# A 4096³ matmul by Strassen-Winograd products: partial sums handed on inside PSUM by ScalarE's copies, and the fifth product put ahead of the fourth

## The chip, the cores and the metric

The kernel runs on one core of one Trainium2 chip. The metric is the device time of one execution in microseconds (us), lower is better. A core has TensorE (PE in the profile: matmuls into the eight banks of PSUM, each 128 partitions x 512 fp32), VectorE (DVE), ScalarE (ACT), GpSimd (POOL) and SyncE (SP). SP, ACT and POOL also start transfers; each starts its own in order.

## The reference

```python
def reference(a, b, alpha):          # a, b: 4096 x 4096 fp32; alpha = 0.01
    x = np.matmul(a, b)
    return np.where(x > 0, x, alpha * x)
```

A full fp32 product followed by a leaky ReLU. The kernel brings a and b in as fp16 (the cast is done by GpSimd's transfers), multiplies with fp32 accumulation, and writes fp32. It also measures row norms on the way and makes a verdict (`good`, later read as `even`) on whether its method was accurate enough; if not, a plain bf16 matmul behind `tc.If(even == 0)` is run instead. For the data here it is not.

## The kernel before, in words

The output is 16 regions of 1024 x 1024. The first is made by plain matmuls during the start. The other 15 are visited in the order (0,1) (0,2) (0,3) (1,2) (1,0) (1,3) (1,1) (2,2) (2,0) (2,3) (2,1) (3,2) (3,0) (3,1) (3,3), where the first number is the row group g and the second the column group j. Each is made by one level of Strassen-Winograd: with a's and b's parts of the region cut into 2 x 2 blocks (of 512 rows or columns, 2048 deep), seven products instead of eight, with the operands of `PRODUCTS`:

- first a11·b11 and second a12·b21; their sum is the block (0,0) of the region ("u1");
- third s2·t2, added to the first in the same banks ("u2");
- fourth s3·t3 ("v"); fifth s1·t1, sixth a22·t4 and seventh s4·b22.

The s are sums of blocks of a, made once per row group by VectorE (`sum_a`, L562). The t are sums of blocks of b made for every region by VectorE in place (`b_sum`, L592). The results are put together by VectorE's additions from the banks and left through `leaky` (L313) and a store by SP. `add_v` (L1046) adds v to u2.

A product is either plain (`product`, L819: 64 matmuls 128 x 128 by 128 x 512, in four banks `y` or `z`) or is itself made by Strassen-Winograd "in quarters" (`quarter_product`, L762: 7 x 16 matmuls of 256 columns). In quarters it needs sums of its own: T1, T2 and T4 of the b operand (`sums_of_b`, L692 to L696) with T3 made in place (`t3_of_b`, L686), and four sums of the a operand, sx1 to sx4, which are made once per row group, kept in device memory (`kept_q`) and loaded again for each region (`load_sums`, L754; `following` inside the sixth loads those of the seventh on ScalarE's queue).

Which products are in quarters:

- row group 0: none;
- the first region of a later row group, (1,2), (2,2), (3,2): sixth and seventh;
- "regular" regions (`in_fourth`), (1,0) (1,3) (2,0) (2,3) (3,0) (3,1) (3,3): fourth, sixth and seventh; in (2,3), the only one in `FIFTH`, the fifth too (`fifth_in_quarters`), with its sums of s1 kept in `kept_s31` and `kept_q["s1"]`;
- "turning" regions, (1,1) and (2,1), the last of a row group (the next row group's a is brought in): the fourth.

The order of the work is written out by hand in the loop over the regions: every engine's instructions stand in program order, and what an instruction waits for is found from the tiles that it reads and writes. `y` and `z` are banks 0 to 3 and 4 to 7, exchanged from region to region. Products 0, 2 and 4 (as `product` numbers them, from 0) accumulate in y, product 1 goes to z, is added to the copy of y by VectorE (`add(u1, z)`, L1041), and z is then used by the fourth and by the sixth.

b is fetched for the next region i+1 by GpSimd (`fetch_b`, L536) into the tile of the block that the present region has read for the last time: (0,1) after the fourth, (0,0) after the sixth's code, which for (2,0) means that its buffer is free when the fifth product has been issued.

`measure` (squares on ScalarE, L231, and sums on VectorE) is put in at certain places of certain regions: before and after product 0 by `EARLY`, others by `MEASURED`. In the last region, (3,3), `judge` is called in two halves: the first, `next(judged)`, reduces the norms (L624) and moves them between partitions by two small transfers, the second, `good = next(judged)`, makes the verdict out of them with twelve small VectorE instructions (L633 to L640). The seventh product of (3,3) is `seventh_at_the_end`: each quarter product's result goes out as early as it can (L1006, L1023 and L313 on VectorE, L1010 to L1031 on ScalarE), and `even` is read from `good` between them.

In (2,2) and (3,2) T2 of the column group has been kept in device memory and is loaded instead of made (`move_t`, L518, on ScalarE's queue).

## Time and profile before

| | us |
|---|---|
| median of 3 runs | 1534.55 |
| lowest, highest | 1533.07, 1534.74 |
| span of the profiled execution | 1531.4 |
| TensorE busy | 1521.0 (99%) |
| VectorE busy | 1171.2 (76%) |
| ScalarE busy | 428.1 (28%) |
| GpSimd busy | 258.2 (17%) |

The span runs from the first to the last instruction of the profiled execution; for that execution the profile gives no other time, so the span stands for it. The profile's clock of TensorE is full in all of its 40 slices. In its rows "L819" is a line of the kernel before, "out<-in" are the tiles written and read, "ps" is PSUM, "xN" the number of instructions, and in a timeline "[1.40 <-DMA b<-in_b_dram]" tells how long the engine stood before the row and what let it go.

The profile places the regions as follows (end of the preceding region, us): (2,0) 877, (2,3) 969 (with a wait for a load at 977), (2,1) 1060.7, (3,2) 1155.9, (3,0) 1249.4, (3,1) 1341.3, (3,3) 1433.2. A regular region takes 91.9 us.

### The profile page before, as it was taken

Reading aid. Unit: us, or ns where it says so; the run is one execution under the profiler, and the core shown is the slowest. Engines: PE = TensorE matmul, PEld = TensorE weight load, DVE = VectorE, ACT = ScalarE, POOL = GpSimd, SP = SyncE. Lnnn points to the kernel's source line nnn. Section 1 sums busy time; section 2 is a strip of 40 time slices with the busy share of each in tenths; the row PEclk is TensorE's granted clock in tenths of the full one; section 3 lists DMA queues with packets and bytes.
Section 4 is the critical chain, followed back from the end, with each engine's and each line's share of the span. In section 5 each row is a group of like instructions: output and inputs, shape, how many; then the busy total and the mean of one; then the engine's idle time right before and its main releaser. Section 6 shows DMA issues by size and latency. Waiting matters only on the chain. (4 is left out here: it accounts for less than half of the span.)

```text
span 1531.4 us, 21934 instructions
## 1 busy us (share of the span) xinstructions
PE 1521.0 (99%) x8715; PEld 851.5 (56%) x8715; DVE 1171.2 (76%) x1231; ACT 428.1 (28%) x734; POOL 258.2 (17%) x426
## 2 busy tenths in 40 slices
PE   9999999999999999999999999999999999999998
PEld 4444444444446567574544747577544475746656
DVE  4378867766897676768789599688978868687677
ACT  2201334646310213103651130313464103041210
POOL 5641110143202011022220001000331100101000
PEclk9999999999999999999999999999999999999999
DMA  9999995998979999899898939859999892948824
GB/s 248 188 216 200 239 281 168 180 193 176 251 312 257 277 237 276 243 290 246 184 310 279 302 149 231 294 154 343 217 241 297 229 347 70 295 161 189 302 97 140
DMA packets 194258, 356.50 MB, mean 233 GB/s; under 512 B 18913, under 2 KB 132833, under 8 KB 181090
## 3 DMA queue, kind: packets, MB, share of 16 engines
q0 software_dynamic: 119808, 112.22, 46.4%
q1 hardware_dynamic: 67714, 217.22, 38.0%
q10 hardware_dynamic: 6624, 25.56, 4.4%
q8 instruction: 70, 1.15, 0.3%
q14 instruction: 42, 0.34, 0.1%
HBM read 347.61 MB, written 117.44 MB: 304 GB/s over the span
## 5 line engine op out<-in xcount | busy, mean ns | idle before, releaser
L819 PE MATMUL ps<-b,a 128*128 128x512 f16 x2624 | 570.7, 379 | 1.4 <-DMA b<-in_b_dram 1.4
L819 PE MATMUL ps<-b,s 128*128 128x512 f16 x2176 | 475.2, 379 | 0.0
L819 PEld LDWEIGHTS <-a 128*128 128x128 f16 x2624 | 256.7, 98 | 309.3 <-issue 1.7
L819 PEld LDWEIGHTS <-s 128*128 128x128 f16 x2176 | 212.8, 98 | 255.2 <-issue 0.4
L592 DVE TENSOR_TENSOR b<-b 128x4096 f16<-128x4096 f16 x104 | 234.8, 2286 | 46.0 <-DMA b<-in_b_dram 34.1
L536 POOL DMA_DIRECT2D b<-in_b_dram x128 | 94.8, 745 | 879.8 <-PE ps L762 448.2
L832 ACT COPY c<-ps 128x512 f32<-128x512 f32 x164 | 85.0, 596 | 483.2 <-PE ps L819 439.2
L142 DVE STREAM_TRANSPOSE a<-a 128x512 uint32<-128x512 uint32 (+2 forms) x120 | 127.0, 1105 | 78.9 <-DMA a<-in_a_dram 78.9
L133 POOL DMA_DIRECT2D a<-in_a_dram x252 | 137.4, 553 | 245.5 <-ACT junk L611 73.6
L762 PEld LDWEIGHTS <-q 128*128 128x128 f16 x1488 | 145.6, 98 | 16.9
L313 DVE SCALAR_TENSOR_TENSOR c<-c 128x1024 f32<-128x1024 f32 (+2 forms) x123 | 141.8, 1194 | 4.1 <-ACT c L832 3.8
L611 ACT ACTIVATE junk<-a 128x512 bf16<-128x512 f16 x192 | 121.1, 631 | 83.4 <-DMA a<-in_a_dram 78.1
L1041 DVE TENSOR_TENSOR c<-ps,c 128x512 f32<-128x512 f32 x140 | 87.5, 683 | 62.8 <-PE ps L819 51.2
L231 ACT ACTIVATE sq<-b 128x2048 bf16<-128x2048 f16 x64 | 118.4, 1910 | 38.8 <-DVE sq L240 31.0
L762 PEld LDWEIGHTS <-a 128*128 128x128 f16 x1200 | 117.4, 98 | 17.4
L283 PE MATMUL ps<-b,a 128*128 128x512 f16 x512 | 112.2, 379 | 0.5 <-ACT a L380 0.2
L762 PE MATMUL ps<-b,q 128*128 128x256 f16 x816 | 95.6, 273 | 0.0
L762 PE MATMUL ps<-b,a 128*128 128x256 f16 x752 | 88.3, 273 | 0.0
L283 PEld LDWEIGHTS <-a 128*128 128x128 f16 x512 | 49.7, 98 | 60.8 <-issue 1.4
L977 ACT COPY c<-ps 128x512 f32<-128x512 f32 x9 | 5.3, 586 | 255.6 <-PE ps L762 145.8
L762 PEld LDWEIGHTS <-s 128*128 128x128 f16 x672 | 65.7, 98 | 7.6
L762 PE MATMUL ps<-q,q 128*128 128x256 f16 x544 | 64.6, 273 | 0.0
(108 smaller groups left out, 917.0 us busy)
## 6 DMA issues: line engine op xcount, KB each, us to landing
b<-in_b_dram POOLq DMA_DIRECT2D x136, 512.0 KB, 11.8
out_dram<-c SPq DMA_DIRECT2D x240, 256.0 KB, 7.0
a<-in_a_dram POOLq DMA_DIRECT2D x244, 128.0 KB, 5.7
b<-kept_half SPq DMA_DIRECT2D x28, 1024.0 KB, 11.8
b<-kept SPq DMA_DIRECT2D x20, 1024.0 KB, 8.8
q<-kept_qs ACTq DMA_DIRECT2D x40, 512.0 KB, 7.8
s<-kept_s SPq DMA_DIRECT2D x18, 1024.0 KB, 7.6
q<-kept_qa SPq DMA_DIRECT2D x28, 512.0 KB, 7.5
```

What stands on the lines that cost most here:

```text
L133: nc.gpsimd.dma_start(a16[32 * q:32 * q + 32], src.rearrange("(g i) w -> i g w", i=32))
L142: nc.vector.transpose(part.rearrange("p c m e -> p c (m e)").bitcast(U32) .rearrange("p c (g i) -> p g c i", i=32), src[:, :, i * n:(i + 1 ...
L231: nc.scalar.activation(to, self.parts[n], SQUARE)
L283: nc.tensor.matmul(ps, a_cols(at[0, h, u], c, mt, (h, u) == (0, 0)), bt[0, u, nt][:, c, :], start=first, stop=last,)
L313: nc.vector.scalar_tensor_tensor(t, t, alpha, t, op0=MULT, op1=MAX if alpha <= 1 else MIN)
L536: nc.gpsimd.dma_start(t[:, c:c + 4, :], b_rows(j, u, c, 4, nt, g > 0))
L592: nc.vector.tensor_tensor(f(to), f(x0), f(x1), op)
L611: nc.scalar.activation(junk, piece[:, q, :], SQUARE, accum_out=to[:, 4 * n + q:4 * n + q + 1])
L762: nc.tensor.matmul(to[m], xq[:, c // 2, rows, c % 2], yq[:, c, :], start=first and c == 0 and m < banks, stop=c == KC - 1, skip_group_chec ...
L819: nc.tensor.matmul(banks[mt], a_cols(t, c, mt, t is first_a), B(half, nt, k)[:, c, :], start=first and (k, c) == todo[0], stop=(k, c) == t ...
L832: nc.scalar.copy(kept[mt], banks[mt])
L1041: nc.vector.tensor_add(to, bank, to)
```

## The change

- **FIFTH is gone.** `fifth_in_quarters`, `kept_s31` and `kept_q["s1"]` are removed; every fifth product is plain.
- **Seeds.** After product 0, ScalarE copies the four banks y into z (bank to bank), product 1 is accumulated on these (`product(1, z, False)`), and u1 is read out by four ScalarE copies (`keep(z, side)`) instead of VectorE's `add(u1, z)`. In the turning regions of row groups 1 and 2 the sixth product starts in the same way on copies of u2, and is copied back. To give the copies time, the last 16 matmuls of product 0 (and of product 2 in regular regions) and the first 16 of product 1 (and of product 4) run bank by bank.
- **EARLY measures.** Only the first one ends before the copies; others begin after the copies and end after the b sums.
- **Regular regions, order.** Both units of t4, the sixth's operand (made in B(1,0)), are summed after product 1 instead of one of them after product 2; the first of the two units of t1, the fifth's operand (made in B(0,0)), is summed during product 2, followed by T3, T2 and T1 of the fourth, and then the second unit. Then comes product 4 (the fifth, plain, in y) directly after product 2, `fetch_b(i + 1, [(0, 0)])` directly after it, and only then the fourth (`fourth_by_seeds`). `fetch_b(i + 1, [(0, 1)])` stays behind the fourth.
- **Fourth and sixth by seeds.** In both, intermediate sums go from bank to bank by ScalarE's copies (`nc.scalar.copy(one, chain)`), so that VectorE adds 2 parts rather than 5 in the fourth; the quarter products and sums of the sixth stand in another order. The kept sums of a22 are loaded one after product 2, two within the fourth, one near its end.
- **judge.** `good = next(judged)` stands after the sixth instead of before the fifth; T4 for the seventh of (3,3) is made at the end of the sixth; `even` is read one quarter product later.

The loads of T2 in (2,2) and (3,2) are not edited, but stand in program order behind the four seed copies on ScalarE.

```diff
-    FIFTH = {(2, 3)}
-    kept_s31 = dram_pool.tile([P, QUARTER], DT, name="kept_s31")
...
+            if n == 0 or n == 2 and in_fourth:
+                order[-16:] = [(mt, k, c) for mt in range(MT) for k, c in todo[-4:]]
+            elif n == 1 or n == 4 and in_fourth:
+                order[:16] = [(mt, k, c) for mt in range(MT) for k, c in todo[:4]]
             if n == 0 and late_s2:
...
+        def fourth_by_seeds(banks, tq, sx, sq, late):
+
+            pairs, kept = new_c(side)
+            b = quarters_of_b(i, 0, 1)
+            x = quarters_of_a(g, "s3")
+            chain, shared, one, other = banks
             t = lambda n: b_quarter(tq[n])
...
+            quarter_product(x[0, 0], b[0, 0], into(chain), True)
+            nc.scalar.copy(one, chain)
+            quarter_product(sx[1], t(1), into(shared), True)
+            quarter_product(sx[2], t(2), into(chain))
+            nc.scalar.copy(other, chain)
+            quarter_product(x[0, 1], b[1, 0], into(one))
+            nc.scalar.copy(block(0, 0), pair(one))
+            for n in (2, 3):
+                sq[n] = new_a16()
+            load_sums("a22", sq, (2, 3))
+            quarter_product(sx[3], b[0, 1], into(chain))
+            nc.scalar.copy(one, chain)
+            nc.scalar.copy(block(1, 1), pair(chain))
+            quarter_product(sx[4], b[1, 1], into(other))
+            nc.scalar.copy(block(0, 1), pair(other))
+            sq[4] = sq["room"] = late
+            load_sums("a22", sq, (4,))
+            quarter_product(x[1, 1], t(4), into(one))
+            nc.scalar.copy(block(1, 0), pair(one))
+            return pairs, kept, [(block(r, 1), pair(shared)) for r in (1, 0)]
...
+            quarter_product(x[0, 0], b[0, 0], into(chain), True)
+            nc.scalar.copy(one, chain)
+            add(v, y)
+            quarter_product(sx(1), t(1), into(shared), True)
             following(4)
             next_t[2] = tq[1]
...
+            leave(v_pairs, 1, 1)
+            quarter_product(sx(2), t(2), into(chain))
+            nc.scalar.copy(other, chain)
             following(2)
...
             sums_of_b(y7, next_t, (2,))
...
+            quarter_product(x[0, 1], b[1, 0], into(one))
+            more(0, 0, one)
+            for r in (0, 1):
+                more(r, 1, shared)
+            next_t[4] = tq[2]
+            if not final:
+                sums_of_b(y7, next_t, (4,))
+            quarter_product(sx(3), b[0, 1], into(chain))
+            nc.scalar.copy(one, chain)
+            more(1, 1, chain)
+            following(1, sq.get("last"))
             quarter_product(sx(4), b[1, 1], into(other))
...
             more(0, 1, other)
+            following(3, sq.get("room"))
+            quarter_product(x[1, 1], t(4), into(one))
             more(1, 0, one)
...
+            sums_of_b(y7, next_t, (1, 4) if final else (1,))
             return next_t, next_s
...
             leaky(block(0, 0))
-            even = nc.values_load(good[0:1, 0:1], min_val=0, max_val=1)
             quarter_product(sx(2), t(2), ones)
...
             leaky(block(0, 1))
+            even = nc.values_load(good[0:1, 0:1], min_val=0, max_val=1)
             quarter_product(sx(3), b[0, 1], ones, by_row=True)
...
         product(0, y, True)
...
+        for m in early[:1]:
             m.end()
+        for mt in range(MT):
+            nc.scalar.copy(z[mt], y[mt])
+        for m in early[1:]:
+            m.begin()
...
-        product(1, z, True)
+        product(1, z, False)
...
-        add(u1, z)
+        u1_pairs, _ = keep(z, side)
         leave(u1_pairs, 0, 0)
...
         for k in ks:
             b_sum(B(0, 0, k), B(1, 1, k), B(0, 0, k), SUB)
+            if in_fourth and k == ks[0]:
+                tq = {n: new_a16() for n in (2, 1)}
+                y7 = quarters_of_b(i, 0, 1)
+                t3_of_b(y7)
+                sums_of_b(y7, tq, (2, 1))
...
+            sq = {1: new_a16()}
+            load_sums("a22", sq, (1,))
+            product(4, y, False)
+            fetch_b(i + 1, [(0, 0)], ks)
+            t3_of_b(y6)
+            sums_of_b(y6, t6, (2, 1))
+            t3_of_b(quarters_of_b(i, 1, 1))
+            v_pairs, v, parts = fourth_by_seeds(z, tq, {**s3_rooms(g), 4: a_quarter(sx4)}, sq, t[:, 3])
+            for to, bank in parts:
+                nc.vector.tensor_add(to, bank, to)
+            add_v()
+            tq = t6
+            sums_of_b(y6, tq, (4,))
...
-        if final and not in_fifth:
-            good = next(judged)
...
-            product(4, y, False)
+        if not in_fourth:
+            product(4, y, False)
...
+            tq, sq = sixth_in_quarters(u2_pairs, banks, v_pairs, v, y, tq, sq)
+            if final:
+                good = next(judged)
...
-            product(5, z, g > 0)
-            add(u2[::-1], z[::-1])
+            product(5, z, False)
+            if g:
+                for mt in range(MT):
+                    nc.scalar.copy(u2[mt], z[mt])
+            else:
+                add(u2[::-1], z[::-1])
```

More of the change, by code (lines that the diff above doesn't have):

```diff
@@ L846, in fourth_in_quarters @@
             nc.scalar.copy(block(0, 0), pair(one))
-            if not turning:
-                quarter_product(sx[4], b[1, 1], into(other), True)
             quarter_product(x[1, 1], t(4), into(third), True)
@@ L907, in sixth_in_quarters @@
+        def sixth_in_quarters(pairs, banks, v_pairs, v, y, tq, sq):
             b = quarters_of_b(i, 1, 0)
             x = quarters_of_a(g, "a22")
-            one, other, third, fourth = banks
+            chain, shared, one, other = banks
             t = lambda n: b_quarter(tq[n])
@@ L1104 @@
             keep_s2(g)
-        if i and regions[i - 1] in FIFTH:
-            for c in range(KC // 2):
-                nc.sync.dma_start(by_chunk(x21(g, "a22"))[:, c], by_chunk(kept_s31)[:, c])
         product(0, y, True)
@@ L1121 @@
                 move_t("t2", t, k, False, nc.scalar)
-        u1_pairs, u1 = keep(y, side)
         if middle:
@@ L1136 @@
             middle.end()
+        for m in early[1:]:
+            m.end()
         if g == 1 and j in OTHERS:
```

168 lines of the change are left out of this document (26 added, 142 removed).

## The prediction

> **What bounds the kernel now.** I read the page first, then TensorE's waits, the chain of waits that ended last, and VectorE's timeline over the last region. The page:
>
> ```profile
> span 1531.4 us, 21934 instructions
> PE 1521.0 (99%) x8715; PEld 851.5 (56%) x8715; DVE 1171.2 (76%) x1231; ACT 428.1 (28%) x734; POOL 258.2 (17%) x426
> PEclk9999999999999999999999999999999999999999
> ```
>
> TensorE works through 99% of the span at full clock. A change can only gain by fewer matmul columns or by the few microseconds in which TensorE stands; it can lose in every new wait. TensorE's waits, with total, count and longest in us:
>
> ```profile
> PE ps L819 <- DMA b<-in_b_dram: 1.4, 1, 1.4
> PE wp L106 <- DVE x L92: 1.2, 1, 1.2
> ...
> ```
>
> The second, and two more that are not shown (each smaller), belong to the start. Only the first is in the range of the change. The chain says what it is (start, length, what):
>
> ```profile
> 945.38 33.41 DMA b<-in_b_dram
> 978.79 0.04 issue
> 978.84 32.97 PE ps L819 x152
> 1011.80 48.94 PE ps L762 x448
> ...
> 1114.41 110.51 PE ps L819 x512
> ...
> 1433.23 41.44 PE ps L819 x192
> 1474.67 12.23 PE ps L762 x112
> 1486.90 13.81 PE ps L819 x64
> 1500.71 22.72 PE ps L762 x208
> ...
> 1525.77 0.42 DVE c L313
> ```
>
> After the load that lands at 978.79 (B(0,0) of region (2,3)) there is no gap on TensorE up to 1523. Here are the prices too: a plain product of 64 matmuls is 13.81 us, one in quarters (112 matmuls of half the width) 12.23 us, so one quarter product is 12.23 / 7 = 1.747 us. From 978.84 on, L762 x448 is four products in quarters in a row: the fourth to seventh of (2,3).
>
> **The change, part by part.** The sum is made against the profiled execution of 1531.4 us; the median of the runs, 1534.55, stands 3.15 us above that span, and I add the sum to the median.
>
> *The fifth of (2,3) becomes plain.* 13.81 − 12.23 = +1.58 us on TensorE, which nothing covers. With it go 4 stores and 4 loads of s1's sums, the kept part of s3, and some VectorE work that covered nothing on the path: no gain from them.
>
> *The fetch of the next B(0,0) moves up.* GpSimd's timeline:
>
> ```profile
> 944.65 1.48 POOL L536 DMA_DIRECT2D b<-in_b_dram  x2 [5.43 <-PE ps L819]
> ```
>
> The pair could issue only when the fifth product, the last reader of B(0,0), was nearly through. The fifth now stands ahead of the fourth, so the pair issues about 12.2 us earlier. Even with the same 33.4 us in flight it lands near 967, ten before the need at 977.4: −1.4 us. The (0,1) pair, which went out ahead of it, now goes after the fourth, about 12 to 14 later; it is first read by the sums for the third product, so 33 us in flight still suffice.
>
> *Seeds from product 0 to 1.* In each of 15 regions four ScalarE copies put y into z, product 1 accumulates on them, and four copies out replace four VectorE additions. The rows for these:
>
> ```profile
> L832 ACT COPY c<-ps 128x512 f32<-128x512 f32 x164 | 85.0, 596 | 483.2 <-PE ps L819 439.2
> L1041 DVE TENSOR_TENSOR c<-ps,c 128x512 f32<-128x512 f32 x140 | 87.5, 683 | 62.8 <-PE ps L819 51.2
> 876.60 18.73 PE L819 MATMUL ps<-b,a 128*128 128x512 f16 x86
> 885.07 1.91 ACT L231 ACTIVATE sq<-b 128x2048 bf16<-128x2048 f16 x1 [1.79 <-DVE sq L240]
> 888.27 7.31 ACT L231 ACTIVATE sq<-b 128x2048 bf16<-128x2048 f16 x4 [1.29 <-DVE sq L243]
> 895.49 2.03 ACT L832 COPY c<-ps 128x512 f32<-128x512 f32 x4
> ```
>
> No row shows a copy from bank to bank; its nearest is bank to SBUF, .596 each and four in 2.03, and I take that. The last 16 matmuls of product 0 and the first 16 of product 1 go bank by bank, so bank m ends 4 × .216 = .86 us after bank m−1 and is wanted .86 after its neighbour: every copy has about 3 × .86 = 2.6 us, in regions that keep the order by pairs of banks about 1.7, against .6 plus handing over. Cost 0; if a copy took 1.1 us, the second pair's two would end 1.1 and 2.2 after product 0 and be wanted at 1.73 and 2.59: still in time. The danger is ScalarE's other work: in (2,0), whose product 0 (876.60 + 13.81) ends at 890.4, the copies of y stood behind eight squares of `measure`, 5.1 us late, and as seeds they would hold TensorE for that long. But the changed kernel ends only the first measure ahead of the copies (squares to 886.98) and begins the second (888.27) behind them; the first pair of banks is complete at about 887.0. That VectorE has four additions of .683 fewer gains nothing: TensorE doesn't wait for it there.
>
> *Fourth by seeds.* The same 112 matmuls, with three bank-to-bank copies, each having one quarter product (1.747) to hide in .6. Cost 0. Its a22 quarters are loaded later: two right after the fourth's third and second operands are through, one at its end, each about 10.4 us ahead of its use. Median landing of such loads:
>
> ```profile
> q<-kept_qs ACTq DMA_DIRECT2D x40, 512.0 KB, 7.8
> q<-kept_qa SPq DMA_DIRECT2D x28, 512.0 KB, 7.5
> DMA to landing us min/median/max: 3.0/7.8/11.1
> ```
>
> So 0 at the median, up to .7 at the maximum.
>
> *Sixth by seeds.* VectorE's timeline in region (3,3) gives the spacings, here and for the tail (two additions of 512 columns in 1.29, so .60 apart; a half-size sum 1.13 apart; two leaky ReLU in 2.35):
>
> ```profile
> 1488.14 0.36 DVE L624 TENSOR_REDUCE ends<-stats 128x2 f32<-128x32 f32 x3
> ...
> 1494.34 2.35 DVE L1046 TENSOR_TENSOR c<-c 128x1024 f32<-128x1024 f32 x2
> 1496.61 0.59 DVE L633 TENSOR_REDUCE most<-line 1x2 f32<-1x256 f32 x1
> ...
> 1499.65 0.15 DVE L640 TENSOR_TENSOR good<-ok 1x1 int32<-1x1 f32 x1
> 1500.10 1.29 DVE L1041 TENSOR_TENSOR c<-ps,c 128x512 f32<-128x512 f32 x2 [0.30 <-PE ps L819]
> ...
> 1513.60 1.22 DVE L696 TENSOR_TENSOR q<-b,q 128x2048 f16<-128x2048 f16 x1
> 1514.73 2.36 DVE L313 SCALAR_TENSOR_TENSOR c<-c 128x1024 f32<-128x1024 f32 x2
> 1517.00 0.75 DVE L1006 TENSOR_TENSOR c<-ps,c 128x256 f32<-128x256 f32 x2
> ...
> 1520.02 1.29 DVE L1023 TENSOR_TENSOR c<-ps,c 128x512 f32<-128x512 f32 x2 [1.54 <-DMA out_dram<-c]
> ```
>
> In the sixth the margin is thin. Its seventh quarter product accumulates on the bank that ScalarE may overwrite only after VectorE has read it (`more(0, 0, one)`). VectorE has other work ahead of that read. Counted from the sixth's start, and with those spacings: the second half of `add_v` can begin at .83, once the fourth's last copy (.6) is out, and ends at 1.96; T4 3.1; four additions of y at .60 each 5.5; the leaky ReLU of v (2 × 1.13) 7.77; T2 8.9; the read 9.5. ScalarE's copy ends at 10.2, and TensorE arrives at 6 × 1.747 = 10.48. Margin .2 to .3, in six regions: cost 0, up to .5 each if one link is longer.
>
> *T2 loads of (2,2) and (3,2).* They stand on ScalarE's queue behind the four seeds, and so go out only after product 0:
>
> ```profile
> 1167.18 0.33 ACTq L518 DMA_DIRECT2D b<-kept_t  x1
> 1169.69 0.33 ACTq L518 DMA_DIRECT2D b<-kept_t  x1
> DMA to landing us min/median/max: 4.8/8.9/12.0
> ```
>
> Region (3,2) starts three plain products after the chain's 1114.41, at 1155.85; its product 0 ends at 1169.67 and product 2 reads them at 1183.5; leaving at about 1170.9 behind the seeds, with 12.0 in flight, they land at 1182.9. Cost 0, with little to spare at the maximum.
>
> *The turning regions' sixth product* starts on seeds from u2: four more copies within product 5's 13.81. Cost 0.
>
> *The tail.* In region (3,3) the verdict of `judge` (`good = next(judged)`) moves from before the fifth's end to behind the sixth, ahead of the leaky ReLU of u2. In the rows above, twelve small instructions from 1496.61 to 1499.80 are 3.2 us that VectorE had free. On TensorE:
>
> ```profile
> 1500.55 1.91 PE L762 MATMUL ps<-b,a 128*128 128x256 f16 x16
> ...
> 1512.78 3.66 PE L762 MATMUL ps<-b,s 128*128 128x256 f16 x32
> ```
>
> It starts the sixth at 1500.55 and the seventh 12.23 later, at 1512.78. VectorE reads y's first two banks at 1517.00 to 1517.75 (L1006); TensorE's fifth quarter product of the seventh (`onto(0, 1)`) writes these banks at 1512.78 + 4 × 1.747 = 1519.77: a margin of 2.0.
>
> After the change, counted from the sixth's start, VectorE has: `add_v`'s second half from .83 to 1.96; T4 to 3.10; L624 .28, to 3.38; four additions of y 2.4, to 5.78; leaky of v 2.27, to 8.04; T2 to 9.17; five additions from banks at .6, to 12.2; the sixth waits for the last quarter product, 12.49 to 13.09; T4 and T1 2.26, to 15.35; judge 3.22, to 18.57; leaky of u2 2.27, to 20.84; L1006 twice, to 21.6. TensorE would want the banks at 12.23 + 6.99 = 19.22, so it stands about 2.4. VectorE's rest (two more pairs, L1023, four leaky, four additions, about 7.3 with no room between) ends at 28.57, against 1526.19 − 1500.55 = 25.64 before. The end comes +2.93 us later; the last stores follow as before. Bounds: 0 if VectorE is not the bound, 3.2 if all of judge shows, plus some tenths for the later `values_load`.
>
> Sum: 1.58 − 1.4 + 2.93 = +3.1 us: 1534.55 + 3.1 = 1537.7.
>
> One rule of the skill bears on the new stall. The trace: TensorE's 1.4 us wait at 977.4 left the clock at 9 in every slice, and at the start 11 matmuls of 512 columns took 4.11 us, .37 each, where 64 in 13.81 later take .216:
>
> ```profile
> 1.19 4.11 PE L106 MATMUL wp<-w 128*128 128x512 f16 x11 [1.19 <-DVE x L92]
> ```
>
> The Trainium skill, "TensorE: Matmul & The Clock Gate", section "What's actually happening", says that the clock halves after an idle window of some 3.4 us. By it a stall of 2.4 costs itself alone, and the sum stays; one longer than 3.4 would have the rest at half speed.
>
> **The rivals.**
>
> *A, forecast:* the tail is late, the rest is hidden: 1537.7, from 1536.6 to 1538.6.
>
> *B, new waits in the regular regions besides.* For it: margins of .2 to .3 in the sixth, of .7 for the loads, in six or seven regions. Against it: VectorE is at 76%, and the waits need the slow end of their rows. At .3 to .5 in seven regions: +2.1 to +3.5, 1539.8 to 1541.2.
>
> *C, the other side: the tail is covered.* If VectorE reads y's first two banks within 6.99 us of the seventh's start, then TensorE doesn't stand and the end stays: 1.58 − 1.4 = +.2, 1534.7. It decides at 2.4 us less on VectorE between the sixth's start and that read, for instance if the additions to u2 come one quarter product earlier than I count. Against: each term is a row of this same region.
>
> *D, the clock falls in the tail.* A stall beyond 3.4 us, with the last three quarter products (5.24) at half speed: +1 +5.2, 1543.9. It needs a stall one us longer than worked out.
>
> *E, faster:* the 1.4 us are got back, more stalls that I don't see go too, and the tail is covered. TensorE's only other gaps are the start's; there is nothing to win 3 us from.
>
> **How the numbers follow.** 0.2% is 3.07 us, about what a measurement of this kernel can tell from no change: the bounds are 1531.5 and 1537.6. Chances: A .53, B .20, C .21, D .03, E .03. A lies on the upper bound, so I give it half and half, .25 same and .28 slower; B and D are slower, C is the same: faster .03, same .46, slower .51. The range goes from C, 1534.5, to B's upper end, 1541.0.
>
> **What would show it.** TensorE's busy time from 8715 to 8667 matmuls, and the wait of 1.4 for b<-in_b_dram gone; a wait of about 2.4 us of TensorE for VectorE's additions to c in the last 10 us; judge's twelve small instructions (L633 to L640) some 15 us into the sixth and the seventh; VectorE's last leaky ReLU about 3.1 later than 1525.77 + .42. Wrong would be: TensorE waits for ScalarE at product 1, or for the copies in the sixth, or for q<-kept_qa, in several regions (B); no wait in the tail (C); a granted clock under 9 in the last slice (D).

## The result, and the profile after

The changed kernel takes 1536.79 us (median of 20 runs, 1536.40 to 1538.65). The kernel before takes 1532.39 us over 20 runs made beside them (1531.29 to 1538.32), lower than each of the three runs that the prediction could see (they are among the 20). The ratio is 1.0025 with a 95% interval of 1.0018 to 1.0032, so the change makes the kernel slower by 3.8 us (2.8 to 4.9; 4.4 by the medians). Predicted were +3.1 us.

The first lines of the page after:

```profile
span 1535.9 us, 21828 instructions
PE 1523.3 (99%) x8667; PEld 846.8 (55%) x8667; DVE 1093.0 (71%) x1104; ACT 495.6 (32%) x857; POOL 258.2 (17%) x426
```

VectorE has 78 us less to do, ScalarE 67 us more, and TensorE 2.3 us more in its records (48 matmuls fewer, but wider). TensorE's waits after (total, count, longest in us):

```profile
PE ps L758 <- DVE c L977: 1.6, 1, 1.6
PE turned L373 <- DVE a_rounded L357: 1.2, 1, 1.2
...
PE ps L283 <- DVE a L142: 0.8, 1, 0.8
```

The wait of 1.4 for b<-in_b_dram is gone. One of 1.6 for VectorE is new. The other two lie in the first 100 us, in the region of the start, whose code the change leaves alone; the wait of 0.8 varies from profile to profile (0 to 1.2 in those below). The chain's end, in which no wait stands between regions any more:

```profile
1434.39 55.25 PE ps L819 x256
1489.64 22.71 PE ps L758 x208
1512.38 1.91 PE ps L758 x16
1514.31 7.16 PE ps L758 x64
1521.47 1.20 DVE c L313
```

55.25 us are now four plain products in a row (the fifth ahead of the fourth), and at 1521.47 the chain leaves TensorE for VectorE, where before it stayed on TensorE up to 1523.43. TensorE's and VectorE's timelines there:

```profile
1501.70 1.91 PE L758 MATMUL ps<-b,a 128*128 128x256 f16 x16
...
1514.31 3.65 PE L758 MATMUL ps<-b,s 128*128 128x256 f16 x32
1517.80 3.66 PE L758 MATMUL ps<-q,q 128*128 128x256 f16 x32
1523.06 3.87 PE L758 MATMUL ps<-b,q 128*128 128x256 f16 x32 [1.60 <-DVE c L977]
```

```profile
1510.99 4.03 DVE L900 TENSOR_TENSOR c<-ps,c 128x512 f32<-128x512 f32 x6
...
1517.20 0.59 DVE L633 TENSOR_REDUCE most<-line 1x2 f32<-1x256 f32 x1
...
1520.25 0.15 DVE L640 TENSOR_TENSOR good<-ok 1x1 int32<-1x1 f32 x1
1520.33 2.34 DVE L313 SCALAR_TENSOR_TENSOR c<-c 128x1024 f32<-128x1024 f32 x2
1522.60 0.73 DVE L977 TENSOR_TENSOR c<-ps,c 128x256 f32<-128x256 f32 x2
...
1529.44 0.42 DVE L313 SCALAR_TENSOR_TENSOR c<-c 128x256 f32<-128x256 f32 x1
```

From 1501.70, the sixth's start, VectorE has no pause until the end of L977. The verdict (L633 to L640) begins 15.5 us after that start, and the leaky ReLU of u2 can follow only at 1520.33; TensorE, which could have gone on at 1521.30, starts its fifth quarter product of the seventh at 1523.06.

The whole difference of the two profiled executions (1535.9 − 1531.4 = 4.5 us) can be laid out by three points of each trace: the sixth's start in (3,3), VectorE's last instruction, and the end of the span.

| | sixth's start | to VectorE's end | from there to the end | span |
|---|---|---|---|---|
| before | 1500.55 | 25.64 | 5.2 | 1531.4 |
| after | 1501.70 | 28.16 | 6.0 | 1535.9 |
| difference | +1.15 | +2.52 | +0.8 | +4.5 |

The first term lies in the start: the first matmul of L819 begins at 120.51 us before and at 121.77 after, and in the other profiles anywhere from 120.42 to 122.31. From there to the sixth's start the two take 1380.0 and 1379.9 us, so that the plain fifth and the lost wait cancel. The second term is the tail that the prediction has. The third is not in its sum (its bounds allow some tenths for the later reading of `even`). In the experiments below, profiles that keep the tail of the kernel before have 4.2 to 4.9 us there, those that keep the changed kernel's have 5.9.

A run's time is longer than its span, and not by the same amount in each kernel: by 1.9 us in the 20 runs of the changed kernel (median span 1534.9), by 2.5 to 3.0 us, as medians, in the four sets of runs of the kernel before that stand beside the experiments (median spans 1529.6 to 1530.3). In spans the change therefore costs some 5 us, in time 3.8 to 4.4. What fills the part outside the span is not in the traces.

### The profile page after: what moved, and what is told of

It is laid out like the page before. It is cut to its first block, busy times and chain, and to the rows that moved or that the text cites. A ratio compares the mean times of both kernels' runs of the same rounds, so it can differ in the third digit from the quotient of the medians.

```text
span 1535.9 us, 21828 instructions
## 1 busy us (share of the span) xinstructions
PE 1523.3 (99%) x8667; PEld 846.8 (55%) x8667; DVE 1093.0 (71%) x1104; ACT 495.6 (32%) x857; POOL 258.2 (17%) x426
## 3 DMA queue, kind: packets, MB, share of 16 engines
q8 instruction: 70, 1.15, 0.3%
## 4 chain that ended last, share of the span: by engine, by line
PE 96%; DMA 2%; DVE 1%; POOL 1%; issue 0%; ACT 0%; SPq 0%; DVEq 0%
PE ps L819 68%; PE ps L758 23%; PE ps L283 4%; DMA a<-in_a_dram 1%; DMA b<-in_b_dram 1%; POOL b L193 0%; DMA a_in<-in_a_dram 0%; POOL a L133 0%; DVE a L142 0%; DVE c L977 0%; DVE c L313 0%; PE turned L373 0%; DVE c L993 0%; DVE a L380 0%; DVE part L320 0%
## 5 line engine op out<-in xcount | busy, mean ns | idle before, releaser
L819 PE MATMUL ps<-b,a 128*128 128x512 f16 x2624 | 570.6, 379 | 0.0
L819 PE MATMUL ps<-b,s 128*128 128x512 f16 x2240 | 488.0, 379 | 0.0
L819 PEld LDWEIGHTS <-a 128*128 128x128 f16 x2624 | 256.7, 98 | 307.7
L819 PEld LDWEIGHTS <-s 128*128 128x128 f16 x2240 | 219.2, 98 | 263.8
L536 POOL DMA_DIRECT2D b<-in_b_dram x128 | 94.8, 745 | 873.3 <-PE ps L819 402.2
L832 ACT COPY c<-ps 128x512 f32<-128x512 f32 x164 | 86.0, 596 | 285.6 <-PE ps L819 273.0
L758 PEld LDWEIGHTS <-q 128*128 128x128 f16 x1424 | 139.3, 98 | 18.1 <-issue 2.0
L758 PE MATMUL ps<-b,q 128*128 128x256 f16 x784 | 92.0, 273 | 1.7 <-DVE c L977 1.6
L1080 ACT COPY ps<-ps 128x512 f32<-128x512 f32 x60 | 32.8, 572 | 163.0 <-PE ps L819 163.0
L1184 DVE TENSOR_TENSOR c<-ps,c 128x512 f32<-128x512 f32 x14 | 9.7, 691 | 105.8 <-ACT c L878 102.2
L1012 DVE TENSOR_TENSOR c<-ps,c 128x512 f32<-128x512 f32 x72 | 44.5, 679 | 45.8 <-PE ps L819 45.8
L758 PE MATMUL ps<-q,q 128*128 128x256 f16 x640 | 73.1, 273 | 0.0
```

The source lines that it names most:

```text
L536: nc.gpsimd.dma_start(t[:, c:c + 4, :], b_rows(j, u, c, 4, nt, g > 0))
L758: nc.tensor.matmul(to[m], xq[:, c // 2, rows, c % 2], yq[:, c, :], start=first and c == 0 and m < banks, stop=c == KC - 1, skip_group_chec ...
L819: nc.tensor.matmul(banks[mt], a_cols(t, c, mt, t is first_a), B(half, nt, k)[:, c, :], start=first and (k, c) == todo[0], stop=(k, c) == t ...
L832: nc.scalar.copy(kept[mt], banks[mt])
L1012: nc.vector.tensor_add(to, bank, to)
```

## The experiments

Each run's time stands beside runs of the kernel before on the same chip.

### The fifth product made plain, and nothing else

```diff
-    FIFTH = {(2, 3)}
+    FIFTH = set()
```
(on the kernel before)

> The kernel before with FIFTH empty and nothing else: the fifth of (2,3) becomes plain. My theory: 13.81 - 12.23 = +1.6 us, nothing hides it, and the wait of 1.4 us for B(0,0) stays: 1534.0 where the kernel before has 1532.4. The rival: the quarters' additions and loads cost as much somewhere as they save on TensorE: 1532.4.

Measured: 1532.88 us, ratio 0.9996 (0.9988 to 1.0005). The rival has it: the same time. TensorE's wait of 1.4 us is gone in this profile too, although here the fetch of B(0,0) stands where it stood. The rows for its four transfers in the kernel before and in this one are the last lines of two views of line L536, between 937 and 948 us:

```profile
DMA to landing us min/median/max: 16.5/25.9/33.4
```

```profile
DMA to landing us min/median/max: 6.3/9.1/12.4
```

They are issued 0.65 us apart in the two traces, and the last lands in 12.4 us instead of 33.4. What else is on its way at that time in the kernel before, on SyncE's queue:

```profile
929.15 7.04 SPq L710 DMA_DIRECT2D kept_qs<-q  x4
936.61 6.43 SPq L754 DMA_DIRECT2D q<-kept_qa  x4
```

The four stores of 512 KB are the sums of s1 that the quartered fifth of (2,3) needs. Without it they aren't made, and the loads behind them go out earlier. So in these two profiles the quartered fifth saves 1.58 us in (2,3) and costs as much at the start of the same region (1.4 us of wait, 1.56 in the spacing of TensorE's matmuls). Which of the transfers that go away or go earlier had slowed the pair, this run does not separate.

The wait is not the same in every execution. In the profile of the run with the late verdict below, whose edit does not touch it, it is 3.2 us. The shortest span of the kernel before is 1528.8 us, as short as that of the last run below, in whose profile this wait is gone, while the shortest here is 1530.4. By these spans (an estimate, since only one execution of each kernel has a trace) the fastest executions of the kernel before have no such wait and keep the 1.58 us. The times do not show it, since here they exceed the spans by 2.0 us, and by 2.8 in the runs of the kernel before beside them.

### The fetch of B(0,0) put back

```diff
             product(4, y, False)
-            fetch_b(i + 1, [(0, 0)], ks)
             t3_of_b(y6)
...
-        if not in_fourth:
-            fetch_b(i + 1, [(0, 0)], ks)
+        fetch_b(i + 1, [(0, 0)], ks)
```

> The changed kernel with the fetch of the next region's B(0,0) put back behind the sixth's code, so that it stands behind the (0,1) pair on GpSimd's queue. My theory: the wait of 1.4 us at the start of (2,3)'s product 0 comes back, or a longer one, 1.4 to 3 us: 1538.2 to 1539.8. The rival (the wait went because other loads went, not because this fetch goes out earlier): no wait, 1536.8.

Measured: 1644.85 us, ratio 1.0725. The direction is as expected, the size is not: 108 us. Of these 78.0 are waits of TensorE for b, and TensorE is busy for 30.6 us longer (1553.9 instead of 1523.3), at a mean granted clock of 0.972 instead of 0.999. The changed kernel's GpSimd in (2,0), then TensorE's wait in this run and the landing of the pairs issued between 970 and 978 us:

```profile
926.67 1.48 POOL L536 DMA_DIRECT2D b<-in_b_dram  x2 [71.32 <-DVE b L684]
933.58 1.48 POOL L536 DMA_DIRECT2D b<-in_b_dram  x2 [5.43 <-PE ps L819]
942.56 2.98 POOL L536 DMA_DIRECT2D b<-in_b_dram  x4 [7.50 <-PE ps L758]
```

```profile
PE ps L819 <- DMA b<-in_b_dram: 78.0, 19, 6.4
```

```profile
DMA to landing us min/median/max: 5.3/27.4/50.0
```

With the fourth behind the fifth, the (0,1) tiles come free only near the region's end, and in program order the (0,0) transfers now stand behind them. Eight transfers go out within 6 us and the last takes 50 us to land. In the changed kernel the (0,0) pairs go out 16 and 9 us before the (0,1) pairs, and nothing waits. The new order of the products therefore depends on the new place of the fetch, even though that place was not needed to lose the old 1.4 us.

### Two tries with an early verdict

In the first, both halves of `judge` are moved ahead:

```diff
+            if final:
+                judged = judge(b_pool.tile([1, P * 6], FP32, name="line", tag="b12"))
+                next(judged)
             product(4, y, False)
...
             t3_of_b(quarters_of_b(i, 1, 1))
+            if final:
+                good = next(judged)
             v_pairs, v, parts = fourth_by_seeds(...)
...
-            if final:
-                good = next(judged)
```

> The changed kernel with both halves of judge moved ahead: the first half before the fifth product of (3,3), the verdict before the fourth's additions, where VectorE stands idle for 15.49 us. My theory (the tail: 3.2 us of judge ahead of the leaky ReLU of u2 hold VectorE, and through the banks TensorE): TensorE's wait of 1.6 us at the end goes, VectorE ends 2.5 to 3.4 us earlier, and the time is 1533.4 to 1534.3 where the changed kernel has 1536.8. The rival (the extra time comes from new waits in other regions, or from the start): the time stays within 0.5 of 1536.8.

Measured: 1536.96 us, ratio 1.0021 (1.0012 to 1.0029): as the rival has it, but for another reason. VectorE and TensorE in this run:

```profile
1500.38 0.60 DVE L633 TENSOR_REDUCE most<-line 1x2 f32<-1x256 f32 x1 [15.64 <-DMA line<-lines]
```

```profile
1504.96 3.65 PE L758 MATMUL ps<-q,q 128*128 128x256 f16 x32 [0.97 <-DVE c L1189]
...
1515.54 1.91 PE L758 MATMUL ps<-q,a 128*128 128x256 f16 x16 [1.69 <-ACT ps L925]
```

The tile `line` takes the room of a b tile that the fourth reads to its end, so its transfer waited for the fourth, and VectorE stood for 15.64 us in front of the verdict. The 3.2 us fell on the sixth instead of the seventh: TensorE waits at 1504 and 1514 and no longer at 1521. The second try gives `line` another room:

```diff
-                judged = judge(b_pool.tile([1, P * 6], FP32, name="line", tag="b12"))
+                room = x_pool.tile([P, 4, QUARTER], DT, name="q", tag="x")
+                judged = judge(room[:1, 0, :P * 12].bitcast(FP32))
```

> As the first run with an early verdict, but the small transfer of judge goes to a tile that is free when the fifth product ends (in the first run its tile was still held by the fourth product, so the verdict came at 1500.38 and held the sixth). The verdict now falls in VectorE's idle time. My theory (judge at the tail costs all of VectorE's delay): no wait of TensorE for VectorE in the last 40 us, VectorE ends 25.6 us after the sixth's start instead of 28.2, and the time is 1533.4 to 1534.5. The rival (the tail's cost is in the sixth's new order, and not in judge): TensorE doesn't wait, but the end stays within 0.7 of the changed kernel's 1536.8.

Measured: 1534.12 us, ratio 1.0008 (0.9999 to 1.0017), within the expectation of the theory and 2.7 us below the changed kernel. Two rows of VectorE:

```profile
1490.67 0.60 DVE L633 TENSOR_REDUCE most<-q 1x2 f32<-1x256 f32 x1 [6.85 <-DMA q<-lines]
...
1516.46 2.35 DVE L313 SCALAR_TENSOR_TENSOR c<-c 128x1024 f32<-128x1024 f32 x2
```

The verdict lies in idle time, TensorE doesn't wait anywhere after the start, and VectorE ends 25.75 us after the sixth's start at 1501.16, 0.1 us more than in the kernel before. The tail of the prediction is judge, and not the sixth's new order.

### The verdict made twice, and half again

```diff
+        for again in range(2):
+            good = verdict(by, again)
+        yield good
...
```

> The changed kernel with the verdict's twelve small instructions made twice, so 3.2 us more on VectorE at the same place. If judge is on the path that sets the end: TensorE's wait at the end grows from 1.6 to about 4.9 us, and the time by 3.2 to about 1540.0. If it is not on it: 1536.8. If TensorE's clock falls after a stall of this length, as the Trainium skill, TensorE: Matmul & The Clock Gate, section What's actually happening, has it for an idle window of some 3.4 us: the three quarter products after the stall (5.24 us) take up to twice as long, and the time is up to 1545.

Measured: 1542.53 us, ratio 1.0051 (1.0037 to 1.0064). The time grows by 4.0 us (by the ratios) to 5.7 (by the medians) over the changed kernel's, and not by 3.2. TensorE, and its clock in a stretch of 3.3 us behind the wait (the column after POOL's busy time):

```profile
1526.62 5.54 PE L763 MATMUL ps<-b,q 128*128 128x256 f16 x32 [4.71 <-DVE c L982]
```

```profile
1527.30:1530.60 3.30, 3.30 (x18) 2.36 (x16) 2.27 (x5) 0.00 (x0) 0.00 (x0) 0.50 0.46 169
```

32 matmuls take 5.54 us instead of 3.66, and the granted clock is 0.50: to the 3.2 us of the verdict comes a slower clock behind a stall of 4.9. VectorE ends 4.6 us later after the sixth's start than in the changed kernel, so the clock costs about 1.4. A stall between this one and the changed kernel's 1.8 is made by repeating only the verdict's three reductions:

```diff
-        for t, n, op in ((most, 0, MAX), (least, 1, MIN), (total, 2, ADD)):
-            nc.vector.tensor_reduce(t, by[:, n], axis=X, op=op)
+        for again in range(2):
+            for t, n, op in ((most, 0, MAX), (least, 1, MIN), (total, 2, ADD)):
+                nc.vector.tensor_reduce(t, by[:, n], axis=X, op=op)
```

> The changed kernel with the verdict's first three reductions made twice: 1.57 us more on VectorE at the tail, so that TensorE's stall there is about 3.3 us, between the 1.8 us after which its matmuls kept their spacing and the 4.9 us after which 31 of them took twice as long. If the stall alone counts: the time grows by 1.6, to 1538.4. If a stall shorter than the 3.4 us of the Trainium skill, TensorE: Matmul & The Clock Gate, section What's actually happening, is enough, as the wait of 2.2 us in the kernel before with the late verdict has it: some 15 to 31 matmuls at .213 instead of .109 us, and 1540 to 1542.

Measured: 1538.67 us, ratio 1.0036 (1.0022 to 1.0049).

```profile
1523.79 5.54 PE L759 MATMUL ps<-b,q 128*128 128x256 f16 x32 [3.17 <-DVE c L978]
```

The time fits the first expectation (1538.4) and the trace the second: the clock falls here too, and 32 matmuls take 5.54 us. In the profile VectorE ends 31.25 us after the sixth's start, 3.1 later than in the changed kernel, 1.6 of it for the reductions and 1.5 for the clock; but only 4.1 us follow instead of 6.0, by which time SyncE has long taken its branch (at 1525.5). (The wait of 2.2 us that the expectation names is in the run that follows.)

### The kernel before with the late verdict

```diff
-        if final and not in_fifth:
-            good = next(judged)
...
             tq, sq = sixth_in_quarters(...)
+            if final:
+                good = next(judged)
```

> The kernel before with the verdict alone moved behind the sixth. Its leaky ReLU of u2 then ends at about 1520.2 instead of 1517.0, TensorE's fifth quarter product of the seventh waits about 1.2 us for VectorE, and VectorE ends about 1.8 us later: 1534.3 where the kernel before has 1532.5 (1533.7 to 1535.6). If judge is not what delays the tail: 1532.5.

Measured: 1535.98 us, ratio 1.0028 (1.0016 to 1.0040): the direction is right, and the size is 3.7 us by the medians instead of 1.8. TensorE's waits and two rows of its timeline:

```profile
PE ps L819 <- DMA b<-in_b_dram: 3.2, 1, 3.2
PE ps L762 <- DVE good L640: 2.1, 1, 2.1
...
PE ps L762 <- DVE q L694: 0.7, 1, 0.7
```

```profile
980.76 9.40 PE L819 MATMUL ps<-b,a 128*128 128x512 f16 x35 [3.20 <-DMA b<-in_b_dram]
...
1523.10 2.48 PE L762 MATMUL ps<-q,q 128*128 128x256 f16 x16 [2.08 <-DVE good L640]
```

In the kernel before, `even` is read out of `good` between the second and the third quarter product of the seventh, and TensorE reads it too. So TensorE waits for `good` itself, ahead of the banks that I had in mind: 2.1 us. That wait was enough for the clock to fall:

```profile
1524.30:1527.50 3.20, 3.20 (x17) 2.27 (x15) 1.88 (x4) 0.65 (x2) 0.00 (x0) 0.50 0.62 221
```

That would be a reason to read `even` a step later, as the change does; no run has the changed kernel with the reading at its old place. The profile's own 1539.9 us hold a longer wait at 978 as well (3.2 us, followed by a stretch at half clock: 35 matmuls in 9.40 us, .27 each).

### When the branch is taken

With the verdict early and clear, VectorE ends as in the kernel before, but in its profile 6.4 us go by from there to the end of the span, against 5.2. SyncE's rows at line 1305 (the branch on `even`) in that run, and its last stores in it and in the kernel before:

```profile
L1305 SPq EVENT_SEMAPHORE  x8: 17/17/17, 1523.6 to 1524.1; - x8
...
L1305 SPq COMPARE_BRANCH  x1: 50/50/50, 1520.9 to 1520.9; - x1
```

```profile
1524.29 4.08 SPq L1339 DMA_DIRECT2D out_dram<-c  x4
```

```profile
1523.11 3.44 SPq L1393 DMA_DIRECT2D out_dram<-c  x4
```

From the branch at 1520.9 to SyncE's next instruction at 1523.6 pass 2.7 us. The Trainium skill, "Runtime: NRT & Kernel Launch", section "Instruction fetch mechanics", has it that a branch to a place outside the prefetched instructions waits until these are fetched; the gap fits that, though no run shows the fetch. The first store's data was ready at 1523.8, and it left at 1524.29. The test reads `even` earlier:

```diff
-            even = nc.values_load(good[0:1, 0:1], min_val=0, max_val=1)
...
+        if final:
+            even = nc.values_load(good[0:1, 0:1], min_val=0, max_val=1)
         leave(u2_pairs, 1, 0)
```

> The run with the early, clear verdict, and even is read out of good before the stores of u2 instead of between the quarter products of the seventh. In that run SyncE read good for 0.75 us behind u2's stores, branched for 2.6 us, and issued the first of the last stores 0.5 us after its data was ready; the last store left 0.7 us after VectorE's last instruction. My theory (the branch on SyncE's queue is what the changed tail still costs beside judge): the last stores go out as VectorE ends, and the time falls by 0.5 to 1.0 us from 1534.1 to about 1533.3, within 1 us of the kernel before. The rival (what is left comes from the start or from transfers): 1534.1 stays.

Measured: 1533.13 us, ratio 1.0002 (0.9993 to 1.0011), as the theory has it, 1.0 us below the run before it. The two intervals overlap, so the number alone does not settle it; the profile agrees, with 4.4 us from VectorE's end to the end of the span. In the changed kernel this path was longer still: u2's stores leave later by the whole delay of the leaky ReLU, and SyncE reads, branches and stores behind them, so that its last four stores begin at 1528.18, 1.3 us after the first one's data (the leaky ReLU of 1526.15) could have gone:

```profile
1528.18 2.46 SPq L1338 DMA_DIRECT2D out_dram<-c  x4
```

The other try on this path starts from the early, clear verdict (the "run before it" of its expectation) and cuts the last four stores in halves:

```diff
-    for to, t in last:
-        nc.sync.dma_start(to, t)
+    for n, mts in ((0, (0, 1)), (1, (0, 1)), (1, (2, 3)), (0, (2, 3))):
+        for mt in mts:
+            to, t = last[mt]
+            cols = slice(n * HALF, (n + 1) * HALF)
+            nc.sync.dma_start(to[:, cols], t[:, cols])
```

> As the run before it, with the last four stores of 256 KB made as eight of 128 KB, in the order in which their halves are finished. If the time after VectorE's last instruction (5.2 us in the kernel before, 6.0 in the changed one) depends on the size of the last store: about 1 us less, 1532.4 to 1533.5. If it is a fixed latency: the same as the run before it.

Measured: 1535.87 us, ratio 1.0022 (1.0012 to 1.0031). Neither expectation: by the medians it is 1.75 us slower than with whole stores, though the two intervals overlap. VectorE ends as early (25.75 us after the sixth's start), but 7.0 us go by behind it instead of 6.4. SyncE takes .35 us and more for each store (median .56), so that the last of the eight goes out 4.1 us after VectorE's last instruction, where the last of the four goes out after 0.7. That explains 0.6 of the 1.75 us; the rest stays open.

### The seeds of product 1 undone

```diff
-        for mt in range(MT):
-            nc.scalar.copy(z[mt], y[mt])
+        u1_pairs, u1 = keep(y, side)
...
-        product(1, z, False)
+        product(1, z, True)
...
-        u1_pairs, _ = keep(z, side)
+        add(u1, z)
```

> The changed kernel with the seeds of product 1 undone alone: y is copied out by ScalarE, product 1 starts afresh in z, and VectorE adds z to the copy (4 additions of 0.68 in each region). My theory, that handing the banks on by copies costs TensorE nothing: within 0.5 of the changed kernel's 1536.8, or up to 1 us more where VectorE's 2.4 us per region make a sum late. The rival, that the seeds hold TensorE: 1534 to 1536.

Measured: 1538.29 us, ratio 1.0035 (1.0022 to 1.0048), 1.5 us above the changed kernel (the intervals overlap) and half a microsecond beyond the range of my theory; the rival, that the seeds hold TensorE, falls. If undoing them costs something, part of it is that VectorE's 2.4 us in each region come back in front of a sum that the fifth product of (2,0) needs:

```profile
PE ps L819 <- DVE b L592: 0.4, 1, 0.4
```

That wait is .4 of the 1.5 us. From the first matmul of L819 to the sixth's start in (3,3) this profile takes .6 us longer than the changed kernel's. The rest stays open.

### The kernel before without its wait, and with the fifth in quarters

If the wait of 1.4 us came from traffic, the kernel before could keep the quarters and lose the wait:

```diff
-            fetch_b(i + 1, [(1, 0)], (1, 0) if in_quarters else ks)
+            if not s1_here:
+                fetch_b(i + 1, [(1, 0)], (1, 0) if in_quarters else ks)
         leave(u2_pairs, 1, 0)
+        if s1_here:
+            fetch_b(i + 1, [(1, 0)], (1, 0))
```

> The kernel before with one transfer moved: in (2,0) the loads of the next region's B(1,0) from kept_half (2 MB) go behind the stores of u2. The fifth of (2,3) stays in quarters. My theory (the wait of 1.4 us came from traffic: the four stores of s1's sums and these loads slow the last pair of B(0,0), 33.4 us in flight where it takes 12.4 us without the stores): the pair lands before its need, the wait goes, and the time falls by 1.5 us to about 1530.8, below both kernels. The rival (the kept stores alone decide, or the wait moves to B(1,0)): the time stays at 1532.3 or grows.

Measured: 1532.40 us, ratio 0.9995 (0.9986 to 1.0004). The last pair of B(0,0) lands in 28.3 us instead of 33.4, in time, and the wait at 978 is gone. But TensorE now waits in (2,1):

```profile
PE ps L762 <- DVE q L694: 1.8, 1, 1.8
```

VectorE makes T4 there behind transposes of the next row group's a, which wait for transfers; TensorE comes 1.4 us earlier and meets it. One more move puts the last of these transposes behind T2, T4 and T1:

```diff
-        if g:
-            bring_a(0, 0, [3])
+        if turning and g:
+            fetch_a(0, 0, 3)
...
             sums_of_b(quarters_of_b(i, 0, 1), tq, (2, 4, 1))
+            turn_a_in(0, 0, 3)
```

> The run with the later half loads, in whose profile the wait at 978 was gone but TensorE waited 1.8 us at 1104 in (2,1) for T4 of the fourth (VectorE, L694), plus one more move: in the turning regions (1,1) and (2,1) the last transposes of the next row group's a (L142, 2.1 us) go behind T2, T4 and T1 of the fourth. If the gain at 978 was lost at 1104 alone: T4 is ready 2.1 us earlier, no wait is left, and the time is 1530.8, below both kernels. If it is lost again further on (the later squares on ScalarE, or the next pieces of a): 1532.4 stays.

Measured: 1532.90 us, ratio 1.0002 (0.9993 to 1.0012). In its profile no wait of TensorE is left outside the first 100 us, and the span is 1530.3, the shortest of all. The median does not follow. Whether other executions of it meet waits that this profile lacks isn't known. No version was found that beats the kernel before by more than the measurement can tell.

## Why the prediction was right

The time came out inside the range, 0.9 us under the point, and the direction was the one with the most weight. That the point is so near is partly luck. Its base, the median of three runs, was 2.2 us above the median of twenty, and its sum was too small by 0.7 (by the ratio) to 1.3 us (by the medians); the two errors have opposite signs. The sum was also read off traces and added to a time, as if time and span grew alike; the part of the time outside the span shrank by about 1 us instead. By the steps of the sum:

- **The fifth of (2,3) becomes plain, +1.58, and the 1.4 us wait goes.** The two terms have the right size in the profiles and cancel: from the first matmul of L819 to the sixth's start in (3,3) the kernel before and the run with FIFTH empty both take 1380.04 us. That the wait is there in every execution was taken from one profile, and the spans speak against it. The causes were wrong. I wrote that the stores and loads of s1's sums which go away bring no gain, and credited the wait to the earlier fetch. The run shows the reverse: with the fetch at its old place and those transfers gone, the same pair lands 21 us sooner. The step that failed is "some VectorE work that covered nothing on the path: no gain from them", which costed removed transfers at nothing without asking which transfer they had slowed.
- **The fetch moved up, −1.4.** It gains nothing in itself, and without it the new order of the products costs 108 us. I had asked what the fetch gains at its new place, and not what the new order makes of the old one.
- **Seeds from product 0 to 1, and in the fourth: 0.** Right. TensorE doesn't wait for ScalarE at any of these seeds: four plain products in a row take 55.25 us, 4 × 13.81. A copy from bank to bank, for which the trace before had no row, takes .57 us where .596 was assumed:

```profile
L1080 ACT COPY ps<-ps 128x512 f32<-128x512 f32 x60 | 32.8, 572 | 163.0 <-PE ps L819 163.0
L907 ACT COPY ps<-ps 128x512 f32<-128x512 f32 x10 | 5.7, 570 | 50.8 <-PE ps L758 50.8
```

- **Sixth by seeds: a margin of .2 to .3, cost 0.** Right, and as thin as worked out. In (3,0), ScalarE's copy ends at 1327.61 + .57 = 1328.18, and TensorE takes the bank at 1328.32, a margin of .14:

```profile
1327.61 0.57 ACT L925 COPY ps<-ps 128x512 f32<-128x512 f32 x1 [3.77 <-DVE c L900]
```

```profile
1328.32 1.91 PE L758 MATMUL ps<-q,a 128*128 128x256 f16 x16
```

Only in (3,3), with L624 in between, TensorE is held, by some .2 us. That settles rival B: no waits in the regular regions.

- **T2 loads, turning regions: 0.** Right by the list of waits.
- **The tail, +2.93.** The mechanism is the one described, and the early, clear verdict removes it. VectorE's times agree nearly to the tenth: judge from 15.5 (worked out: 15.35) to 18.6 (18.57) after the sixth's start, L977's end at 21.6 (21.6). TensorE's wait was 1.8 instead of 2.4, because its first matmul needs only the first of the two banks, and because TensorE itself came .4 late. VectorE's end is 2.52 later, not 2.93.
- **"The last stores follow as before."** This step failed. The branch and the last stores on SyncE follow u2's stores, which the same 3.2 us delay: .8 us in the profile, 1.0 in the run that moves the reading of `even`. It is the term the sum lacked, and with it the tail costs 3.3 us.
- **Rivals C and D.** C (the tail is covered, +.2) is what the two early moves make of the kernel (1533.13), and not what the changed kernel does. D (the clock falls) did not happen at 1.8 us. But the condition that I gave, a stall beyond 3.4 us, was too high: 2.1 us of wait were enough in one run, so the 2.4 that I had worked out could have brought it on. The sign that I named for D, a digit under 9 in the last slice, could not have shown it: a slice is 38 us long, and the page of the run with the verdict twice has 9 in all 40, with 3.4 us at 0.50 in its trace.

The steps that were measured add up to +0.2 (the fifth and the wait) and +3.3 (the tail), 3.5 us of span. The two profiles differ by 4.5, of which 1.3 lie in the start; the median spans differ by about 5, the times by 3.8 to 4.4. So the tail is the cause that the runs show, and 1 to 2 us of the span stay open (the quartered fifth's 1.58 us, in executions without the wait, would be of that size), as does why the time grew less than the span.

## What to carry to other kernels

A small chain of work that is moved for convenience should be priced at the place where it lands: 3.2 us of VectorE that cost nothing in an idle stretch cost nearly all of their length in the last 30 us, on TensorE, VectorE and SyncE's queue together. Before costing removed or moved transfers at nothing, look which transfers share their time and how near those are to being late. And when an order of products is changed, the free moments of buffers move with it, so that every fetch queued in program order has to be looked at again.

## What the runs showed that was not expected

- **TensorE's clock falls after shorter stalls than 3.4 us, and where the stall lies counts.** In the profiles here, waits of 1.4, 1.6, 1.7 and 1.8 us left the granted clock alone. Waits of 2.1 (kernel before, late verdict), 3.2 (twice) and 4.7 us were each followed by 3.4 us at 0.50, which began 0.7 to 1.2 us after TensorE had resumed, and in which a matmul of 256 columns took .213 us instead of .109. The Trainium skill, "TensorE: Matmul & The Clock Gate", section "What's actually happening", names an idle window of about 3.4 us. The length of the slow stretch agrees with that figure, the stall that is needed does not: the shortest here is 2.1 us (one profile). The delay behind the stall is no rule either. In the run with the fetch put back, whose waits reach 6.4 us, half clock begins between 3.2 us before and 0.5 us after TensorE resumes, and lasts 3.4, 6.8 or 13.7 us. In every trace the clock changes only at points that lie whole multiples of 3.41 us apart. What tells the cases apart is how long TensorE is busy between two such points, by the profile's modelled ends. Over the fourteen traces, the 19 stretches at full clock with 1.35 us of work or less were each followed by half clock, and none with 1.44 us or more was. Three of them, with TensorE's busy time behind the length, from the verdict made twice (the second one was followed by half clock, the first was not) and from the late verdict (followed by half clock):

```profile
1520.46:1523.87 3.41, 1.45 (x14) 1.15 (x12) 3.07 (x15) 0.28 (x2) 0.00 (x0) 1.00 0.00 0
1523.88:1527.29 3.41, 0.61 (x5) 0.41 (x5) 3.38 (x6) 0.00 (x0) 0.00 (x0) 1.00 0.41 153
```

```profile
1520.86:1524.27 3.41, 1.33 (x13) 1.04 (x11) 3.13 (x12) 0.00 (x0) 0.00 (x0) 1.00 0.01 2
```

A wait of about 2.1 us (an estimate: 3.41 less 1.35) is thus enough if it falls into one such stretch, and a longer one that is divided between two need not be.
- **A transfer's time in flight depends steeply on what goes out beside it.** The same 512 KB (L536) landed in 12.4, 28.3, 33.4 and 50.0 us, with issue times in the region that differ by a few microseconds.
- **Smaller last stores did not make the end earlier.** By the medians it came 1.75 us later (the intervals overlap), and in the profile the last of eight stores left SyncE 4.1 us after VectorE's last instruction, against 0.7 for the last of four.
